# Nine warm-up products, the last LayerNorm shared by three engines, and the third residual scale in quarters behind FFN2's groups 2 to 5

## The chip, the cores and the metric

The kernel runs on one NeuronCore of a Trainium2 chip. The metric is the device time of one execution in microseconds (us). Engines are named as in the profile: PE is TensorE, DVE is VectorE, ACT is ScalarE, POOL is GpSimd, SP is SyncE, which here only issues DMAs. L246 is line 246 of the kernel; lines behind 380 shift by 3 to 8 in the changed kernel.

## The reference

One layer on 256 tokens of width 2048, in float32. Four blocks follow each other, each with a residual and a LayerNorm behind it:

```python
h = LN(alpha*h + 0.5*SwiGLU_1(h))                  # D_FF = 5504
h = LN(alpha*h + mixer(h))                         # chunked attention and latent attention, gated
h = LN(alpha*h + CrossAttn(h, LN(mem)))            # 4 heads, 256 memory tokens
h = LN(alpha*h + 0.5*SwiGLU_2(h))

def layer_norm(x, g, b):
    mu = x.mean(-1); var = square(x - mu).mean(-1)
    return (x - mu) * rsqrt(var + 1e-5) * g + b
```

## The kernel before, in words

**Products in float32 by halves.** Every float32 operand is split into a rounded half `hi` and a rest `lo`, both of a type that PE takes at full pace. A product is three passes: hi with hi, hi with lo, lo with hi. A weight is loaded in pieces of 128x2048 (1 MB) into one of three raw buffers (`raw`, L182, issued on SP), ACT casts it to `hi` (L243, in pieces of 1024 columns), DVE subtracts to form `lo` (L246). There are two buffers each of `hi` and `lo`; `load` and `halves` (L195 to L247) do this. Activations stand transposed (`T`, `H`, `X` blocks), in halves too, formed by `split` (L235 cast, L236 subtract). A part of the steps is done with sums of weight blocks and of activation blocks, seven products in place of eight (`mm_sums`, L354; the weight sums are L190 and L192 on DVE, from raw into a block named H or X, then cast and subtracted into an X block; the activation sums `sum_forms`, L310 and L314).

**Order.** Steps are put in a list with `add`, each with its weights and a priority; `run` goes through the list, loads weights some steps ahead and emits the instructions. A scheduler then orders each engine's instructions by dependencies and priority: SOON (400) goes ahead of its place in the program, LATE (-400) behind it. On the chip each engine runs its list in that order, and a waiting instruction holds all behind it on its engine.

**FFN.** Eleven groups of 512 hidden columns (the last has 384). A group is eight steps of two 128-row pieces of the input: pairs (L300, 24 products of 512 columns) and sums (L354, 21 products). Gate and up of both token halves fill four PSUM banks; `hidden` (L693) multiplies them, and its `turn` transposes the result on PE (L705) within the next group, whence ACT and DVE bring it to an H block (L235, L236). Groups alternate between the bank pools `mm` and `at`; a group with sums uses banks of both. The first half (groups 0 to 5) is followed by its part of the output projection (`out_pair`), then come groups 6 to 10 and the rest. FFN2's group 0 (`first_group`) is cut up, since the LayerNorm ahead of it comes in between: gate of both halves first, then four `up` steps (L287).

**The residual.** h stands in two tiles (h0, h1), one for each 128 tokens. A LayerNorm writes its normalised h, without scale and offset, back to h, and the transposed form with scale and offset to the T blocks. The scale and offset of the residual itself follow later in `gb_apply` (L434 to L446): for each quarter of 512 columns two row vectors are loaded over all partitions by DMAs of POOL into two of the five 128x512 work tiles `w2`, and DVE multiplies (L445) and adds (L446) for both token halves: four DVE operations of 128x512 and two DMAs a quarter. There are three such passes; the third, `gb_apply(2)`, lies in FFN2 and has to be done before FFN2's output is added.

**Start.** `start` (L470 on) issues 12 products of 128x128 on a tile of ones (L476, results unused), then the first eight steps of FFN1, whose weights and inputs arrive in small pieces.

**End.** The last columns of FFN2's output are made for token half 0, then half 1 (`out_proj` with `cut`; L749, L750, L759). `final_steps` normalises a half: statistics, 1/root by a start value and three steps on 128x1 values (`rsqrt`, L362 to L367), then for each quarter (h - mean)*g (L1361) and *r + b (L1362) on DVE, and the store (L1363) by ACT or SP. Half 0 is done while PE makes half 1; half 1 stands alone at the end.

Of the kernel before, what the change touches and what calls it, by code (L numbers as in the profile page):

```python
# [46 lines left out]
SOON, NEAR, LATE = 400, 100, -400  # L47
WARM = 12
HEADS = ("H4", "H5", "X2", "X3")
# [42 lines left out]
class Kernel:  # L92
# [286 lines left out]

    def ln_scale(self, st):  # L380
        nc = self.nc
        mv, v, y, a = (self.sm(k, n, bufs=2) for k, n in (("mv", 2), ("v", 1), ("y", 1), ("a", 1)))
        nc.vector.bn_aggr(mv, st)
        nc.vector.tensor_scalar(v, mv[:, 1:2], LN_EPS, None, ALU.add)
        self.rsqrt(v, y, a)
        nb = self.sm("nb", 1, bufs=2)
        self.chain = nc.vector.scalar_tensor_tensor(nb, mv[:, 0:1], -1.0, y, ALU.mult, ALU.mult)
        return mv[:, 0:1], y, nb
# [136 lines left out]
    def ffn(self, tag, xT, st, first=None, steps=None, late=None, before=None, tags=None):  # L525
# [6 lines left out]
        for half, nf in enumerate(F_SPLIT):  # L532
# [3 lines left out]
            for g in range(-(-nf // 4)):  # L536
# [15 lines left out]
                hidden, turn = self.hidden(ps, bank, g, n, hid, qs)  # L552
                self.add(hidden, prio=SOON)
                if j == 0 and first is not None:
                    for c in SUMS_IN:
                        self.add(self.forms_step(fx, SUMS_IN, c, xT))
# [93 lines left out]
    def first_group(self, tag, xT, before, ps, fx):  # L650
# [18 lines left out]
        for g in range(4):  # L669
# [5 lines left out]
            self.add(fn, t[tag + "_up"][0, :, g * 2048:(g + 1) * 2048])  # L675
            if g == 0:
                self.add(lambda: self.gb_apply(2, self.h), prio=LATE)
            else:
                self.add(self.forms_step(fx, SUMS_IN, tuple(SUMS_IN)[g - 1], xT))
# [42 lines left out]
    def out_proj(self, wname, nk, x, scale, st, steps=None, tags=None, n0=0, other=False, cut=False):  # L722
# [13 lines left out]
        def part(n, tts, i, ps, tags=None, held=0, keep=False, again=False):  # L736
            grp = groups[i]

            def fn(w=None):
# [12 lines left out]
                for tt in tts:  # L752
# [4 lines left out]
                    if short:  # L757
                        hs = h[tt][:, n * 512:(n + 1) * 512]
                        nc.vector.tensor_tensor(hs, hs, ps[tt], ALU.add)  # L759
                if i == len(groups) - 1:  # L760
# [584 lines left out]
    def final_steps(self, st):  # L1345
# [8 lines left out]
        def steps(tt):  # L1354
            def fn():
                mean, r, _ = self.ln_scale(st[tt])
                g, b = e["gb"]
                for q in range(4):
                    cs = slice(q * 512, (q + 1) * 512)
                    hs = h[tt][:, cs]  # L1360
                    nc.vector.scalar_tensor_tensor(hs, hs, mean, g[:, cs], ALU.subtract, ALU.mult)  # L1361
                    nc.vector.scalar_tensor_tensor(hs, hs, r, b[:, cs], ALU.mult, ALU.add)  # L1362
                    (nc.sync if q % 2 else nc.scalar).dma_start(self.out[0, tt * P:(tt + 1) * P, cs], hs)  # L1363
# [140 lines left out]
```

## Time and profile before

| | us |
|---|---|
| median of 3 runs (2484.69 to 2485.30) | 2485.29 |
| the profiled execution | 2485.13 |
| its span, first to last instruction | 2483.4 |
| PE busy, share of the span | 2467.4, 99% |
| DVE busy | 2066.2, 83% |
| ACT busy | 1337.6, 54% |
| POOL busy | 31.8, 1% |

The profile is of one execution. A timeline row has the start, the duration, the engine, the line, the operation, written tile <- read tiles (buffer numbers left out), the shape and a count when like instructions are merged; behind it stands the idle time of the engine before the row and what ended it. The duration of a merged row reaches from the first start to the last end. Neighbours on one engine overlap by some 0.07 us, so DVE's 128x512 operations of 0.68 us follow each other every 0.6. A row of groups has the busy time, the mean of one in ns, and the idle time before. A row of windows has the length, the busy time of each engine shown with its count, the granted clock of PE, the DMA share and GB/s.

### The profile page before, as it was taken

How to read it: one execution, taken by the hardware profiler on the slowest of the kernel's cores; microseconds unless marked ns; L12 is line 12 of the kernel's file. 1: busy time of each engine (PE TensorE's matmuls, PEld its weight loads, DVE VectorE, ACT ScalarE, POOL GpSimd, SP SyncE). 2: the span in 40 equal slices, each digit the busy share in tenths (PEclk: the TensorE clock that was granted, in tenths of full speed). 3: DMA queues.
4: the chain of work that ended last, by engine and by line, in shares of the span. 5: the costliest groups of instructions: out<-in, count | busy, mean ns of one | idle time of the engine just before them, and what ended most of it. 6: DMA issues, size and time to landing. Idle time of an engine off the chain costs nothing.

```text
span 2483.4 us, 30482 instructions
## 1 busy us (share of the span) xinstructions
PE 2467.4 (99%) x11953; PEld 2079.9 (84%) x11953; DVE 2066.2 (83%) x2334; ACT 1337.6 (54%) x1803; POOL 31.8 (1%) x75
## 2 busy tenths in 40 slices
PE   9999999999999999999999999999999999999998
PEld 8888888889888888899888888888888888888886
DVE  6999889899778988677688798557888988898986
ACT  5555555555455555555455565545545555555552
POOL 0000000000000001000000000000000000000000
PEclk9999999999999999999999999999999999999999
DMA  7655556555645656554566547544655555655663
GB/s 259 240 196 204 187 200 211 203 187 204 237 155 210 212 203 219 178 163 141 172 235 217 189 174 248 189 155 150 209 197 187 203 187 204 210 198 202 203 216 140
DMA packets 72945, 490.16 MB, mean 197 GB/s; under 512 B 8449, under 2 KB 8961, under 8 KB 17633
## 3 DMA queue, kind: packets, MB, share of 16 engines
q1 hardware_dynamic: 67200, 468.29, 54.3%
q0 software_dynamic: 4448, 18.09, 2.2%
q8 instruction: 93, 1.52, 0.2%
q10 hardware_dynamic: 1152, 1.84, 0.2%
q14 instruction: 52, 0.42, 0.0%
HBM read 484.77 MB, written 2.10 MB: 196 GB/s over the span
## 4 chain that ended last, share of the span: by engine, by line
PE 93%; DVE 3%; DMA 2%; ACT 1%; issue 1%; DVEq 0%; ACTq 0%
PE mm L300 26%; PE at L300 24%; PE mm L354 10%; PE at L354 10%; PE mm L266 7%; PE mm L287 5%; PE mm L268 4%; PE mm L256 2%; DVE lo L246 1%; PE at L963 1%; DMA raw<-ffn_w_out_r 1%; PE at L802 1%; DMA raw<-w_xo_r 1%; PE at L1320 0%; PE at L405 0%
## 5 line engine op out<-in xcount | busy, mean ns | idle before, releaser
L243 ACT CAST hi<-raw 128x1024 fp32r<-128x1024 f32 (+1 forms) x848 | 800.9, 986 | 586.1 <-PE at L300 170.5
L246 DVE TENSOR_TENSOR lo<-raw,hi 128x2048 fp32r<-128x2048 f32 (+2 forms) x425 | 902.8, 2125 | 225.0 <-ACT hi L243 220.6
L300 PE MATMUL mm<-hi,T 128*128 128x512 f32 (+1 forms) x1280 | 298.2, 383 | 0.0
L243 ACT CAST X<-H 128x1024 fp32r<-128x1024 f32 (+1 forms) x162 | 165.0, 1034 | 220.4 <-DVE H L192 87.6
L300 PEld LDWEIGHTS mm<-hi,T 128*128 128x128 f32 x1280 | 238.3, 188 | 44.1 <-DVE H L833 0.3
L300 PE MATMUL at<-hi,T 128*128 128x512 f32 x1072 | 257.0, 389 | 0.0
L246 DVE TENSOR_TENSOR X<-H,X 128x2048 fp32r<-128x2048 f32 (+1 forms) x81 | 182.3, 2250 | 67.6 <-ACT X L243 67.6
L300 PEld LDWEIGHTS at<-hi,T 128*128 128x128 f32 x1072 | 201.1, 188 | 41.9
L300 PE MATMUL mm<-lo,T 128*128 128x512 f32 (+1 forms) x640 | 153.8, 382 | 0.0
L300 PE MATMUL at<-hi,H 128*128 128x512 f32 x592 | 140.7, 390 | 0.0
L300 PEld LDWEIGHTS mm<-lo,T 128*128 128x128 f32 x640 | 119.1, 188 | 21.8
L300 PE MATMUL at<-lo,T 128*128 128x512 f32 x536 | 132.6, 389 | 0.0
L300 PEld LDWEIGHTS at<-hi,H 128*128 128x128 f32 x592 | 110.9, 188 | 23.0 <-DVE w L647 0.2
L266 PE MATMUL mm<-T,hi 128*128 128x512 f32 x512 | 124.0, 393 | 0.0
L300 PEld LDWEIGHTS at<-lo,T 128*128 128x128 f32 x536 | 100.6, 188 | 20.9
L300 PE MATMUL mm<-hi,H 128*128 128x512 f32 x464 | 112.3, 392 | 0.0
L192 DVE TENSOR_TENSOR H<-H,raw 128x512 f32<-128x512 f32 (+1 forms) x162 | 109.3, 675 | 1.7
L266 PEld LDWEIGHTS mm<-T,hi 128*128 128x128 f32 x512 | 93.8, 188 | 19.3 <-issue 0.9
L300 PEld LDWEIGHTS mm<-hi,H 128*128 128x128 f32 x464 | 86.2, 188 | 17.6 <-DVE w L275 0.2
L190 DVE TENSOR_TENSOR H<-raw 128x1024 f32<-128x1024 f32 (+1 forms) x81 | 97.1, 1198 | 3.6 <-DMA raw<-ffn_w_in 2.4
L354 PE MATMUL mm<-X,X 128*128 128x512 f32 x348 | 95.7, 391 | 1.7 <-DVE H L236 1.7
L243 ACT CAST X<-raw 128x1024 fp32r<-128x1024 f32 (+1 forms) x54 | 55.3, 1036 | 52.1 <-DVE raw L192 31.5
(332 smaller groups left out, 3946.6 us busy)
## 6 DMA issues: line engine op xcount, KB each, us to landing
raw<-ffn_w_in SPq DMA_DIRECT2D x150, 1024.0 KB, 4.8
raw<-ffn_w_out SPq DMA_DIRECT2D x66, 1024.0 KB, 4.8
raw<-w_gate SPq DMA_DIRECT2D x32, 1024.0 KB, 4.9
raw<-ffn_w_out_r SPq DMA_DIRECT2D x16, 1024.0 KB, 4.9
raw<-w_qk SPq DMA_DIRECT2D x16, 1024.0 KB, 4.8
raw<-w_o_b SPq DMA_DIRECT2D x16, 1024.0 KB, 4.8
raw<-w_out SPq DMA_DIRECT2D x16, 1024.0 KB, 4.8
raw<-w_xk SPq DMA_DIRECT2D x16, 1024.0 KB, 5.0
```

Of the source, the lines that this page charges most:

```text
L190: self.nc.vector.tensor_tensor(two[0], two[1], raw[:, :m].unsqueeze(1).to_broadcast([P, 2, m]), ALU.add)
L192: self.nc.vector.tensor_tensor(t[:, a * m:a * m + m], t[:, b * m:b * m + m], raw[:, a * m:a * m + m], ALU.add)
L243: self.nc.scalar.copy(hi[:, c:d], src[:, c:d])
L246: self.nc.vector.tensor_tensor(lo[:, :n], src, hi[:, :n].bitcast(F32), ALU.subtract)
L256: self.nc.tensor.matmul(ps, w[wi][:, cols[j]:cols[j] + P], x.at(xi, kt), start=(j + wi + xi == 0), stop=(j == n - 1 and wi == 1),)
L266: self.nc.tensor.matmul(ps, hi[kt], x.both(kt), start=(kt == 0), stop=False)
L268: self.last_mm = self.nc.tensor.matmul(ps[:, :S], lo[kt], x.at(0, kt), start=False, stop=(kt == n - 1))
L287: self.last_mm = self.nc.tensor.matmul(ps, x.at(xi, kt)[:, tt * P:(tt + 1) * P], w[wi][:, j * 512 + c:j * 512 + c + m], start=(start and j ...
L300: self.last_mm = self.nc.tensor.matmul(ps[tt, g][:, :n], x.at(xi, kt)[:, tt * P:(tt + 1) * P], w[wi][:, c:c + n], start=first and j + wi + ...
L354: self.last_mm = self.nc.tensor.matmul(bank[:, :m], a[xi], v[wi][:, c * m:(c + 1) * m], start=own and first and wi + xi == 0, stop=own and ...
L802: self.nc.tensor.transpose(ps[:, i * P:(i + 1) * P], s[:, c:c + P], self.ident)
L963: nc.tensor.matmul(ps[:, c0:c0 + nk], q[:, tt * P:(tt + 1) * P], k[:, :nk], start=(j == 0), stop=(j == len(parts) - 1))
```

## The change

Four edits:

- `WARM` goes from 12 to 9.
- `gb_apply(2)` is no longer one step in FFN2's group 0; its four quarters are four steps, each LATE, behind the hidden product of groups 2, 3, 4 and 5.
- In the last LayerNorm the quarters run in the order 2, 3, 0, 1. For token half 1 the quarters 0 and 1 get their (h - mean) from ACT (with -mean as bias) and their *g from POOL; DVE keeps that for 2 and 3, and all four *r + b. -mean is formed ahead of the root, in place of -mean/root behind it, which is unused there.
- The addition of a short product in `out_proj` gets the priority SOON.

```diff
-WARM = 12
+WARM = 9
...
-    def ln_scale(self, st):
+    def ln_scale(self, st, plain=False):
...
         nc.vector.bn_aggr(mv, st)
+        nb = self.sm("nb", 1, bufs=2)
+        if plain:
+            nc.vector.tensor_scalar(nb, mv[:, 0:1], -1.0, None, ALU.mult)
         nc.vector.tensor_scalar(v, mv[:, 1:2], LN_EPS, None, ALU.add)
         self.rsqrt(v, y, a)
-        nb = self.sm("nb", 1, bufs=2)
-        self.chain = nc.vector.scalar_tensor_tensor(nb, mv[:, 0:1], -1.0, y, ALU.mult, ALU.mult)
+        if not plain:
+            self.chain = nc.vector.scalar_tensor_tensor(nb, mv[:, 0:1], -1.0, y, ALU.mult, ALU.mult)
...
                 self.add(hidden, prio=SOON)
+                if before and 2 <= j < 6:
+                    self.add(lambda q=j - 2: self.gb_apply(2, self.h, (q,)), prio=LATE)
...
-            if g == 0:
-                self.add(lambda: self.gb_apply(2, self.h), prio=LATE)
-            else:
+            if g:
                 self.add(self.forms_step(fx, SUMS_IN, tuple(SUMS_IN)[g - 1], xT))
...
                         hs = h[tt][:, n * 512:(n + 1) * 512]
-                        nc.vector.tensor_tensor(hs, hs, ps[tt], ALU.add)
+                        with self.prio(SOON):
+                            nc.vector.tensor_tensor(hs, hs, ps[tt], ALU.add)
...
-                mean, r, _ = self.ln_scale(st[tt])
+                mean, r, nm = self.ln_scale(st[tt], bool(tt))
                 g, b = e["gb"]
-                for q in range(4):
+                for q in (2, 3, 0, 1):
                     cs = slice(q * 512, (q + 1) * 512)
                     hs = h[tt][:, cs]
-                    nc.vector.scalar_tensor_tensor(hs, hs, mean, g[:, cs], ALU.subtract, ALU.mult)
+                    if tt and q < 2:
+                        nc.scalar.activation(hs, hs, AF.Identity, bias=nm)
+                        nc.gpsimd.tensor_tensor(hs, hs, g[:, cs], ALU.mult)
+                    else:
+                        nc.vector.scalar_tensor_tensor(hs, hs, mean, g[:, cs], ALU.subtract, ALU.mult)
                     nc.vector.scalar_tensor_tensor(hs, hs, r, b[:, cs], ALU.mult, ALU.add)
```

What the scheduler makes of it, at three places. First DVE in FFN2's group 0, just behind the last pieces of the transposed LayerNorm (T blocks); h_102 and h_103 are the residual's two halves, w the work tiles. Before:

```order
L236 TENSOR_TENSOR T_2187_14256<-w_2211_14428,T_2187_14256 128x4x128
L414 TENSOR_SCALAR w_2213_14441<-at_14436,vecs 128x128
L445 TENSOR_TENSOR h_102<-h_102,w_2226_14556 128x512
L445 TENSOR_TENSOR h_103<-h_103,w_2226_14556 128x512
L236 TENSOR_TENSOR T_2188_14257<-w_2213_14441,T_2188_14257 128x4x128
L446 TENSOR_TENSOR h_102<-h_102,w_2227_14557 128x512
L446 TENSOR_TENSOR h_103<-h_103,w_2227_14557 128x512
L246 TENSOR_TENSOR lo_14476<-raw_14473,hi_14475 128x2048
L445 TENSOR_TENSOR h_102<-h_102,w_2228_14564 128x512
L246 TENSOR_TENSOR lo_14495<-raw_14492,hi_14494 128x2048
L446 TENSOR_TENSOR h_102<-h_102,w_2229_14565 128x512
```

The same place now:

```order
L236 TENSOR_TENSOR T_2187_14253<-w_2211_14425,T_2187_14253 128x4x128
L417 TENSOR_SCALAR w_2213_14438<-at_14433,vecs 128x128
L314 TENSOR_TENSOR w_2231_14586<-w_2230_14585 128x128 x2
L314 TENSOR_TENSOR w_2231_14586<-w_2231_14586,w_2230_14585 128x128
L310 TENSOR_TENSOR w_2235_14625<-T_2187_14253 128x512
L236 TENSOR_TENSOR T_2188_14254<-w_2213_14438,T_2188_14254 128x4x128
L314 TENSOR_TENSOR w_2231_14586<-w_2230_14585,w_2231_14586 128x128
L314 TENSOR_TENSOR w_2236_14626<-w_2235_14625 128x128 x2
L314 TENSOR_TENSOR w_2236_14626<-w_2236_14626,w_2235_14625 128x128
L310 TENSOR_TENSOR w_2246_14675<-T_2188_14254 128x512
L246 TENSOR_TENSOR lo_14473<-raw_14470,hi_14472 128x2048
```

The sixteen operations on h are gone from there, and the activation sums (L310, L314) have moved ahead of the weights' lo.

Second, DVE in the group behind group 2, now, from the split of its hidden turn (H_2364) on; H_2363 and H_2379 are weight sums:

```order
L236 TENSOR_TENSOR H_2364_15403<-mm_15411,H_2364_15403 128x4x128
L192 TENSOR_TENSOR H_2363_15399<-H_2363_15399,raw_15397 128x512
L246 TENSOR_TENSOR lo_15444<-raw_15397,hi_15443 128x1536
L448 TENSOR_TENSOR h_102<-h_102,w_2349_15320 128x512
L246 TENSOR_TENSOR X_2374_15449<-H_2363_15399,X_2373_15448 128x2048
L246 TENSOR_TENSOR lo_15480<-raw_15477,hi_15479 128x2048
L190 TENSOR_TENSOR H_2379_15486<-raw_15484 128x1024
L246 TENSOR_TENSOR lo_15512<-raw_15484,hi_15511 128x1536
L192 TENSOR_TENSOR H_2379_15486<-H_2379_15486,raw_15484 128x512
L449 TENSOR_TENSOR h_102<-h_102,w_2350_15321 128x512
L192 TENSOR_TENSOR H_2379_15486<-H_2379_15486,raw_15484 128x512
L448 TENSOR_TENSOR h_103<-h_103,w_2349_15320 128x512
```

One more L449 and the next X follow. L448 and L449 are L445 and L446 of before; without these four rows the order there is that of before. Behind groups 3 and 5 it is much the same, behind group 4 two L448 stand ahead of the turn's splits.

Third, the end of DVE, token half 1, from the aggregate of the statistics (mv) on. Before:

```order
L384 TENSOR_SCALAR v_19428<-mv_19427 128x1
L1361 SCALAR_TENSOR_TENSOR h_103<-h_103,mv_19427,T_2876_18715 128x512
L362 TENSOR_SCALAR y_19429<-v_19428 128x1
L1361 SCALAR_TENSOR_TENSOR h_103<-h_103,mv_19427,T_2876_18715 128x512
L363 TENSOR_SCALAR v_19428<-v_19428 128x1
L1361 SCALAR_TENSOR_TENSOR h_103<-h_103,mv_19427,T_2876_18715 128x512
L366 TENSOR_SCALAR a_19430<-y_19429,v_19428 128x1
L1361 SCALAR_TENSOR_TENSOR h_103<-h_103,mv_19427,T_2876_18715 128x512
L367 TENSOR_SCALAR y_19429<-a_19430,y_19429 128x1
```

Now:

```order
L386 TENSOR_SCALAR nb_19429<-mv_19424 128x1
L387 TENSOR_SCALAR v_19425<-mv_19424 128x1
L1369 SCALAR_TENSOR_TENSOR h_103<-h_103,mv_19424,T_2876_18712 128x512
L362 TENSOR_SCALAR y_19426<-v_19425 128x1
L1369 SCALAR_TENSOR_TENSOR h_103<-h_103,mv_19424,T_2876_18712 128x512
L363 TENSOR_SCALAR v_19425<-v_19425 128x1
L366 TENSOR_SCALAR a_19427<-y_19426,v_19425 128x1
L367 TENSOR_SCALAR y_19426<-a_19427,y_19426 128x1
```

Two of the four big operations have left DVE, and nb stands in front. Behind the root four L1370 (L1362 of before) follow in both. The two products are the last work on POOL, and on ACT two activations (L1366) stand between the stores of half 0 and those of half 1. The short addition (L759, now L763) keeps its place behind the four L1370 of half 0.

## The prediction, made before the changed kernel was run

> **What bounds the kernel now.** I read the page first: the engines' shares and the chain that ended last.
>
> ```profile
> span 2483.4 us, 30482 instructions
> PE 2467.4 (99%) x11953; PEld 2079.9 (84%) x11953; DVE 2066.2 (83%) x2334; ACT 1337.6 (54%) x1803; POOL 31.8 (1%) x75
> PE 93%; DVE 3%; DMA 2%; ACT 1%; issue 1%; DVEq 0%; ACTq 0%
> ```
>
> TensorE (PE) is busy for all but 16.0 us of the span. What can be won lies in those 16 us, or in PE instructions that go; what can be lost is any new wait of PE. So the second view is what PE waited for in the whole run (us in total, times, longest).
>
> ```profile
> PE mm L354 <- DVE H L236: 1.7, 1, 1.7
> PE at L476 <- DVE w L452: 1.1, 1, 1.1
> ```
>
> The other waits of PE are 0.6 us and less. Third, the timeline at three places. At the start PE runs the warm-up products and then its first real ones; at the end DVE alone runs the last LayerNorm after PE has stopped at about 2471.7; the 1.7 us wait stands in FFN2. The change touches exactly these three. The sum below is against the profiled execution: span 2483.4, own time 2485.13, which lies 0.16 below the median of 2485.29; the 1.8 us around the span stay.
>
> **Warm-up, 12 products to 9.**
>
> ```profile
> 1.06 5.49 PE L476 MATMUL at<-w 128*128 128x128 f32 x24 [1.06 <-DVE w L452]
> 4.89 1.19 ACT L235 CAST hi<-raw 128x512 fp32r<-128x512 f32 x2 [2.20 <-DMA H<-xT]
> 6.21 0.70 PE L300 MATMUL mm<-hi,T 128*128 128x512 f32 x1
> 6.74 1.09 PE L300 MATMUL mm<-hi,T 128*128 128x512 f32 x4
> 11.99 3.79 PE L300 MATMUL mm<-hi,T 128*128 128x512 f32 x16
> 60.96 1.03 PE L705 MATMUL mm<-ident,w 128*128 128x128 f32 x8
> ```
>
> Twelve products are 24 records, from 1.06 to the first real product at 6.21: 0.21 us each. Products of the same shape later (L705) come 0.11 apart, so PE runs at half pace here. The first real product takes 0.70 us and the next four 1.09 together: full pace came between 6.2 and 6.74. Three products less free 6 x 0.21 = 1.28 us. They are not all gained: the first weights (hi) are ready only when the first of the two casts ends, at 4.89 + 0.6 = 5.5. The products start at about 5.57, not 4.93, so 0.64 us come free, and at half pace they hold half as much work: **0.33 us**. The next inputs come in time for that: the second cast ends at 6.1, needed at 6.6, and the later pieces of the first two units keep 0.2 us or more. From 11.99 on PE runs without a gap, so the 0.33 lasts. Nothing to zero is the other end if the pace rises earlier, since the last warm-up products are then short.
>
> **The third scale and offset (L445, L446) out of FFN2's first group.**
>
> ```profile
> L446 DVE TENSOR_TENSOR h<-h,w 128x512 f32<-128x512 f32 x8 | 5.3, 683 | 0.6 <-DMA w<-gb 0.6
> L445 DVE TENSOR_TENSOR h<-h,w 128x512 f32<-128x512 f32 x8 | 5.2, 682 | 0.0
> 1815.29 1.07 PE L287 MATMUL mm<-lo,T 128*128 128x512 f32 x4
> 1815.99 0.62 ACT L235 CAST X<-w 128x512 fp32r<-128x512 f32 x1 [3.53 <-DVE w L314]
> 1820.94 2.29 DVE L246 TENSOR_TENSOR lo<-raw,hi 128x2048 fp32r<-128x2048 f32 x1 [2.37 <-ACT hi L243]
> 1823.26 0.33 SPq L182 DMA_DIRECT2D raw<-ffn_w_in  x1
> 1829.27 1.23 DVE L190 TENSOR_TENSOR H<-raw 128x1024 f32<-128x1024 f32 x1 [2.42 <-DMA raw<-ffn_w_in]
> 1836.16 1.98 PE L300 MATMUL at<-lo,T 128*128 128x512 f32 x8
> 1841.85 0.39 PE L354 MATMUL mm<-X,X 128*128 128x512 f32 x1
> 1843.19 1.28 DVE L236 TENSOR_TENSOR H<-mm,H 128x512 fp32r<-128x512 f32 x2
> 1843.93 1.66 PE L354 MATMUL mm<-X,X 128*128 128x512 f32 x6 [1.69 <-DVE H L236]
> ```
>
> Between 1795.5 and 1818.6 DVE runs these 16 operations, 10.5 us, and 0.6 us of waiting for their loads. They stand ahead of the sums that ACT waits for (3.53 us), so ACT casts the weights of the last `up` step late, DVE forms their lo late (1820.94), the raw buffer comes free late and the load on SP goes out at 1823.26. DVE then idles 2.42 us for that load and runs without a pause from 1829.27 to the split L236 at 1843.19, whose PSUM bank PE wants 0.23 after 1841.85. That is PE's 1.7 us.
>
> Without the 16 operations the lo at 1820.94 is bound by PE alone. Its buffers come free near 1816.3, when PE ends the step two before (the row at 1815.29), so I put its end at 1820, 3.2 us earlier. The load follows, L190 starts at 1826 to 1826.5, the next lo ends near 1831, and its load is back for the second L190 near 1836. The lo ahead of L236 needs a buffer that PE gives back at 1838.1 (the row at 1836.16); then 2.2 us of it, and the first L236 ends near 1841.5. PE wants the bank at 1842.1. What is late next is that same split, with some 0.6 us to spare: I take **1.7 us** gained, bounds 0 and 1.85 (the whole gap of 2.08 between the two products less the usual 0.23).
>
> **The same operations behind groups 2 to 5.** Four per group, in DVE's pace 4 x 0.6 = 2.4 us. DVE's busy time from one hidden turn to the next:
>
> ```profile
> 1924.80:1967.20 42.40, 39.17 (x39) 1.00 0.56 198
> 1967.20:2009.65 42.45, 38.37 (x34) 1.00 0.60 204
> 2009.65:2052.10 42.45, 38.76 (x38) 1.00 0.50 172
> 1935.03 2.29 DVE L246 TENSOR_TENSOR X<-H,X 128x2048 fp32r<-128x2048 f32 x1 [0.90 <-ACT X L243]
> 1944.77 2.29 DVE L246 TENSOR_TENSOR X<-H,X 128x2048 fp32r<-128x2048 f32 x1 [1.12 <-ACT X L243]
> 1950.25 2.29 DVE L246 TENSOR_TENSOR lo<-raw,hi 128x2048 fp32r<-128x2048 f32 x1 [0.98 <-ACT hi L243]
> 1949.53 0.62 PE L354 MATMUL at<-X,T 128*128 128x512 f32 x2
> ```
>
> Idle are 3.2 to 4.1 us of each group, for 2.4 us of work, and the order puts the work where the idle stands. Behind group 2 the first L445 falls into the 0.90 us before the X at 1935.03. One L446 between the two L192 delays the second by 0.6 us, hence ACT's cast of X and the X at 1944.77 by 0.6. PE reads that X's lo half after 1949.5, when it had been done at 1947.1: 1.8 us are left. The 0.98 us before the lo at 1950.25 take up the rest. So **0**, with the idle as cover; without it 4 x 2.4 = 9.6 us. What stands behind a late L445 on DVE are lo and X, which PE and, through the raw buffer, SP's loads wait for. The loads g and b go out on POOL as before, now two per group. In group 2 the first waits for the turn near 1925 to free its buffer, nine us ahead of its L445; a DVE wait there is possible only in the last quarter, where L446 follows the freed buffer by a few us.
>
> **The tail.**
>
> ```profile
> 2472.80 0.29 DVE L383 BATCH_NORM_AGGREGATE mv<-bn 128x2 f32<-128x30 f32 x1
> 2473.19 0.74 DVE L1361 SCALAR_TENSOR_TENSOR h<-h,mv,T 128x512 f32<-128x512 f32 x1
> 2474.58 0.14 DVE L363 TENSOR_SCALAR v<-v 128x1 f32<-128x1 f32 x1
> 2476.14 0.20 DVE L367 TENSOR_SCALAR y<-a,y 128x1 f32<-128x1 f32 x1
> 2477.25 0.21 DVE L367 TENSOR_SCALAR y<-a,y 128x1 f32<-128x1 f32 x1
> 2477.57 2.73 DVE L1362 SCALAR_TENSOR_TENSOR h<-h,y,T 128x512 f32<-128x512 f32 x4
> L895 ACT ACTIVATE H<-H,ly 128x512 f32<-128x512 f32 x2 | 1.3, 716 | 2.0 <-DVE ly L371 2.0
> L462 POOL MEMSET krope<- 128x512 f32 x1 | 0.5, 515 | 0.0
> masks.py:199 POOL TENSOR_SCALAR_AFFINE_SELECT ident<-ident 128x128 f32<-128x128 f32 x1 | 0.3, 285 | 0.0
> ```
>
> DVE keeps two L1361 and loses two. The two that go stood between the small steps of the root and hid their latency, so less than 2 x 0.66 is won. The new nb in front costs 0.07. v at L363 then stands at 2474.65, its two successors 0.2 and 0.3 later, so the first y of the loop at 2475.15 in place of 2476.14. The last y is 1.11 after it (2476.14 to 2477.25), at 2476.26, and with the old nb gone L1362 starts at 2476.51 in place of 2477.57: 1.06 us. Each L1362 and its store follow as before (0.66 apart, the store 2.1 us from issue to landing), so the end moves as much, if quarters 0 and 1 are ready as third and fourth, by 2477.8 and 2478.5. ACT gets nb at 2473.3 and needs some 0.72 each (L895): 2474.1 and 2474.8. It has nothing queued ahead but the first half's stores, issued by then. POOL multiplies after that. Its product of two inputs stands in no row. Below: a 128x512 memset takes 0.515, so not less; above: the 128x128 select with one input takes 0.285, so four times that for each of two inputs, 2.3. By one pass of 0.41 per stream, two in and one out, it is 0.1 + 3 x 0.41 = 1.3, near the lower rows, and I take 1.3: done at 2475.4 and 2476.7, in time, **1.06**. If POOL and DVE's L1361 and L1362 cannot run beside each other, POOL starts at 2474.7, ends at 2477.3, and the first L1362 waits until then: 0.24 is left. No row shows the two side by side, so I take the middle, **0.65**. At 2.3 each and in turns POOL would end at 2479.3 and DVE at 2482.0: 1.8 lost.
>
> The Trainium skill speaks against this part: "SBUF — State Buffer", section "SBUF: two separate sides", says that a GpSimd operation that reads SBUF and a DVE operation with two SBUF inputs share a port pair as an exclusive lock for the whole instruction. By that rule the tail gives 0.24 and the sum is 2.3; no run here shows it yet.
>
> SOON around the short add moves nothing: DVE's order has that add behind the same four L1362.
>
> **Sum.** 0.33 + 1.7 + 0 + 0.65 = 2.7 us; 2485.1 - 2.7 = **2482.5**.
>
> **Rivals.**
> First, the clock. Full pace may need an unbroken run of PE, and the change leaves a gap of 0.64 us at 4.9. The profile records that idleness takes the pace away:
>
> ```profile
> 2471.70:2474.50 2.80, 0.03 (x1) 0.00 (x0) 2.70 (x8) 0.00 (x0) 0.00 (x0) 1.00 0.13 48
> 2474.50:2480.00 5.50, 0.00 (x0) 0.00 (x0) 5.32 (x15) 0.00 (x0) 0.00 (x0) 0.50 0.15 55
> ```
>
> The granted clock (third from the right) is 0.50 some 2.8 us after PE's last product. Before, full pace came 5.1 to 5.7 us after the first product. Counted anew from 5.57 it comes near 11.1 in place of 6.7, and half of 4.4 us, 2.2, is lost: 2484.7. Against it: PE waited 1.7 us in FFN2 and kept its pace. Chance 20%. The Trainium skill, "TensorE: Matmul & The Clock Gate", Part 1, has a free-running window of about 3.4 us that must be busy; by it one window more costs 1.7 us, 2484.2. The 5.1 to 5.7 us of half pace here agree with one window missed and one kept.
>
> Second, the split L236 stays late in FFN2, since DVE's run of nearly 14 us ahead of it has the same instructions: 1.7 us are not won, 2484.2. The 2.42 us of idle that go speak against it. 10%.
>
> Third, POOL is slow and takes turns with DVE: the tail loses 1.8 instead of gaining 0.65, 2484.9. 12%.
>
> Fourth, on the other side: DVE's late lo and X reach PE in groups 2 to 5. With none of the 9.6 us covered the time is 2482.5 + 9.6 = 2492.1; from 2.7 us uncovered on, the kernel is slower than before. For it: DVE is 90 to 92% busy there, and its idle is itself a wait for ACT, which waits for DVE. Against: no PE wait stands in these groups now, and the slack counted above. 4%.
>
> **The numbers.** The forecast has 54%, with 2481.9 (all bounds good) to 2483.7 as its own range. The range that should hold 8 in 10 takes in the first three rivals: 2481.4 to 2484.9. A measurement of this kernel tells about 0.2% from no change, here 5 us: below 2480.3 lies none of the cases (2% for what I overlook), above 2490.3 only the fourth (4%), so 94% within.
>
> **What would show it.** Right: 18 warm-up records, the first L300 product at 5.5 to 5.6 and its row of 16 at about 11.65 in place of 11.99; no PE wait on L236 near 1841; no PE wait in groups 2 to 5; the last L1362 ending some 7.9 us after PE's last product instead of 8.6. Wrong: L300 rows still 0.43 apart after 7 us, a PE wait on lo or X in FFN2, an idle DVE before the third L1362 with POOL as its releaser.

## The result, and the profile after

The changed kernel takes **2482.48 us** (median of 22 runs, 2481.79 to 2483.96) beside 2485.61 for the kernel before (22 runs, 2483.86 to 2488.49): ratio 0.9986, 95% interval 0.9981 to 0.9992. That is 3.1 us; 2482.5 had been predicted, as 2.7 us less than a before of 2485.1. The profiled execution took 2481.91, its span is 3.3 us shorter than the one of before. From here on, offsets are starts of the same instruction in the two profiles, after less before. Each profile is of one execution.

The page after the change, span, PE and the chain that ended last; then what PE waited for.

```profile
span 2480.1 us, 30475 instructions
PE 2466.1 (99%) x11947; PEld 2078.3 (84%) x11947; DVE 2065.5 (83%) x2332; ACT 1338.7 (54%) x1805; POOL 34.8 (1%) x77
PE 96%; DVE 2%; DMA 1%; ACT 0%; issue 0%; SPq 0%; DVEq 0%; ACTq 0%
```
```profile
PE at L479 <- DVE w L455: 1.1, 1, 1.1
PE mm L300 <- ACT hi L235: 0.7, 2, 0.6
```

The row for the 1.7 us wait on the split L236 is gone. A new wait stands in L300, on hi: that is at the start. PE there, then ACT:

```profile
1.06 3.92 PE L479 MATMUL at<-w 128*128 128x128 f32 x18 [1.06 <-DVE w L455]
5.56 2.96 PE L300 MATMUL mm<-hi,T 128*128 128x512 f32 x10 [0.58 <-ACT hi L235]
8.69 1.66 PE L300 MATMUL mm<-hi,T 128*128 128x512 f32 x6 [0.17 <-ACT hi L235]
12.00 3.79 PE L300 MATMUL mm<-hi,T 128*128 128x512 f32 x16
```
```profile
7.11 0.62 ACT L235 CAST hi<-raw 128x512 fp32r<-128x512 f32 x1 [1.08 <-DMA raw<-ffn_w_in]
8.01 0.62 ACT L235 CAST hi<-raw 128x512 fp32r<-128x512 f32 x1 [0.28 <-DMA raw<-ffn_w_in]
```

The first product starts 0.65 us earlier, but the row of 16 begins at 12.00 (before: 11.99). The next pieces of hi come when their loads land, and PE waits for both casts: of the ten merged products one starts at 7.78, and the row of six at 8.69, each 0.05 to 0.06 us after the end of a cast (7.73, 8.63). **Nothing is gained here.** Full pace came earlier in this execution than in the one of before: the last warm-up records, from 4.6 on, are 0.11 us apart, so the first real products ran at full pace, and all that this and the earlier start gave went into these waits and smaller pauses beside them.

FFN2's first groups, DVE and then PE:

```profile
1825.79 1.22 DVE L190 TENSOR_TENSOR H<-raw 128x1024 f32<-128x1024 f32 x1
1836.17 1.22 DVE L190 TENSOR_TENSOR H<-raw 128x1024 f32<-128x1024 f32 x1 [1.16 <-DMA raw<-ffn_w_in]
1840.97 1.28 DVE L236 TENSOR_TENSOR H<-mm,H 128x512 fp32r<-128x512 f32 x2
```
```profile
1841.71 0.73 PE L354 MATMUL mm<-X,X 128*128 128x512 f32 x2
1843.90 2.44 PE L300 MATMUL at<-hi,T 128*128 128x512 f32 x10
```

The splits are at 1840.97 in place of 1843.19, and PE's product at 1841.71 comes only 0.1 late. It is still that split that releases it: the weight load that goes with it waits for the split, and starts 0.05 us after its end at 1841.66.

```profile
1841.71 0.30 PEld L354 LDWEIGHTS mm<-X,X 128*128 128x128 f32 x2 [0.38 <-DVE H L236]
```

The offset goes from 0.00 at 1838 to -1.76 at 1843.9.

DVE and PE behind groups 2, 3 and 4, as windows that lie within 0.4 us of those before (length, PE, PEld, DVE, ACT, POOL, granted clock, DMA share, GB/s):

```profile
1923.40:1965.85 42.45, 42.45 (x194) 35.22 (x193) 41.60 (x43) 24.43 (x31) 1.08 (x2) 1.00 0.59 210
1965.85:2008.30 42.45, 42.45 (x193) 35.09 (x192) 41.80 (x40) 23.72 (x30) 1.07 (x2) 1.00 0.64 224
2008.30:2050.75 42.45, 42.45 (x193) 35.07 (x192) 39.22 (x37) 23.05 (x28) 1.08 (x2) 1.00 0.59 191
```

DVE has 2.4, 3.4 and 0.5 us more than before, and behind group 5 (2050.3 to 2092.4) 2.2 more; the fullest window leaves it 0.65 us of idle. PE is busy throughout, and the offset stays within 0.1 us from 1850 to 2100: the quarters cost nothing, with less room than before.

The tail, token half 1: ACT, POOL, DVE; then POOL's and DVE's lines by themselves (ns, shortest, median, longest).

```profile
2470.81 1.33 ACT L1366 ACTIVATE h<-h,nb 128x512 f32<-128x512 f32 x2 [17.88 <-DVE nb L386]
2471.62 2.94 POOL L1367 TENSOR_TENSOR h<-h,T 128x512 f32<-128x512 f32 x2 [119.32 <-ACT h L1366]
2470.29 0.29 DVE L383 BATCH_NORM_AGGREGATE mv<-bn 128x2 f32<-128x30 f32 x1
2471.47 0.74 DVE L1369 SCALAR_TENSOR_TENSOR h<-h,mv,T 128x512 f32<-128x512 f32 x1
2473.99 3.10 DVE L1370 SCALAR_TENSOR_TENSOR h<-h,y,T 128x512 f32<-128x512 f32 x4
```
```profile
L1367 POOL TENSOR_TENSOR h<-h,T x2: 1254/1488/1721, 2471.6 to 2473.3; 128x512 f32<-128x512 f32 x2
L1370 DVE SCALAR_TENSOR_TENSOR h<-h,y,T x4: 739/739/1114, 2474.0 to 2476.4; 128x512 f32<-128x512 f32 x4
```

From the aggregate's start to the end of the last multiply-add: 6.80 us, before 7.50 (2472.80 to 2480.30), so **0.70 gained**. POOL's first product, begun while DVE's second L1369 ran, took 1.72, the second 1.25; DVE's first L1370, begun 0.56 us before POOL's second ended (at 2474.56), took 1.11 in place of 0.74.

A fourth place had not been in the prediction: the last loads of FFN2's output. Before, with the DMA view of the first 4 us behind the issue at 2444.52 (queue, kind: packets, MB, share; then the load's KB and time to landing):

```profile
2450.10 1.05 ACT L243 CAST X<-raw 128x1024 fp32r<-128x1024 f32 x1 [3.62 <-DMA raw<-ffn_w_out_r]
2451.06 1.99 ACT L243 CAST hi<-raw 128x1024 fp32r<-128x1024 f32 x2
2453.08 2.29 DVE L246 TENSOR_TENSOR lo<-raw,hi 128x2048 fp32r<-128x2048 f32 x1 [3.67 <-ACT hi L243]
2455.42 1.21 PE L287 MATMUL mm<-lo,H 128*128 128x512 f32 x4 [0.33 <-DVE lo L246]
```
```profile
q8 instruction: 1, 0.02, 1.9%
raw<-ffn_w_out_r SPq DMA_DIRECT2D x1, 1024.0 KB, 5.6
```

And after, the same load, issued at 2442.68:

```profile
2447.56 1.05 ACT L243 CAST X<-raw 128x1024 fp32r<-128x1024 f32 x1 [2.93 <-DMA raw<-ffn_w_out_r]
```
```profile
q1 hardware_dynamic: 127, 1.02, 75.6%
raw<-ffn_w_out_r SPq DMA_DIRECT2D x1, 1024.0 KB, 4.9
```

Before, the load landed 5.6 us after its issue, a transfer of 16 KB of the kind "instruction" fell into its first 4 us, and PE lost 0.6 us from 2454.7 on (gaps of 0.49 and 0.11 beyond the usual spacing): ACT's cast to X waits for the load, its casts to hi stand behind that one, DVE's lo waits for hi, and PE for lo. After, the transfer falls 4.4 us behind the issue, when the load is nearly done; the load takes 4.9 and PE does not wait. The account of the profiled pair: 0 + 1.76 + 0 + 0.6 + 0.70 = 3.06, and 0.2 us of scatter between.

### The profile page after: what moved, and what is told of

It reads as the page before. It is cut to its first block, busy times and chain, and to the rows that moved or that the text cites. A ratio compares the mean times of both kernels' runs of the same rounds, so it can differ in the third digit from the quotient of the medians.

```text
span 2480.1 us, 30475 instructions
## 1 busy us (share of the span) xinstructions
PE 2466.1 (99%) x11947; PEld 2078.3 (84%) x11947; DVE 2065.5 (83%) x2332; ACT 1338.7 (54%) x1805; POOL 34.8 (1%) x77
## 4 chain that ended last, share of the span: by engine, by line
PE 96%; DVE 2%; DMA 1%; ACT 0%; issue 0%; SPq 0%; DVEq 0%; ACTq 0%
PE mm L300 26%; PE at L300 25%; PE mm L354 10%; PE at L354 10%; PE mm L287 7%; PE mm L266 7%; PE mm L268 4%; PE mm L256 2%; PE at L967 1%; PE at L287 1%; PE at L806 1%; PE at L1324 0%; PE at L408 0%; PE at L1300 0%; PE at L1008 0%; PE mm L708 0%
## 5 line engine op out<-in xcount | busy, mean ns | idle before, releaser
L300 PE MATMUL mm<-hi,T 128*128 128x512 f32 (+1 forms) x1280 | 298.7, 383 | 0.8 <-ACT hi L235 0.7
L300 PEld LDWEIGHTS mm<-hi,T 128*128 128x128 f32 x1280 | 237.8, 188 | 46.0 <-ACT hi L235 2.1
L300 PE MATMUL at<-hi,T 128*128 128x512 f32 x1072 | 257.0, 389 | 0.0
L300 PEld LDWEIGHTS at<-hi,T 128*128 128x128 f32 x1072 | 201.1, 188 | 41.9
L300 PE MATMUL mm<-lo,T 128*128 128x512 f32 (+1 forms) x640 | 153.8, 382 | 0.0
L300 PE MATMUL at<-hi,H 128*128 128x512 f32 x592 | 140.7, 389 | 0.0
L300 PEld LDWEIGHTS mm<-lo,T 128*128 128x128 f32 x640 | 119.1, 188 | 21.8
L300 PE MATMUL at<-lo,T 128*128 128x512 f32 x536 | 132.6, 389 | 0.0
L300 PEld LDWEIGHTS at<-hi,H 128*128 128x128 f32 x592 | 110.9, 188 | 22.9
L300 PEld LDWEIGHTS at<-lo,T 128*128 128x128 f32 x536 | 100.6, 188 | 20.9
L300 PE MATMUL mm<-hi,H 128*128 128x512 f32 x464 | 112.3, 392 | 0.0
L300 PEld LDWEIGHTS mm<-hi,H 128*128 128x128 f32 x464 | 86.2, 188 | 17.6 <-DVE w L275 0.2
L190 DVE TENSOR_TENSOR H<-raw 128x1024 f32<-128x1024 f32 (+1 forms) x81 | 97.2, 1200 | 2.1 <-DMA raw<-ffn_w_in 1.2
```

The lines of the kernel that those rows point to most:

```text
L190: self.nc.vector.tensor_tensor(two[0], two[1], raw[:, :m].unsqueeze(1).to_broadcast([P, 2, m]), ALU.add)
L300: self.last_mm = self.nc.tensor.matmul(ps[tt, g][:, :n], x.at(xi, kt)[:, tt * P:(tt + 1) * P], w[wi][:, c:c + n], start=first and j + wi + ...
```

## The experiments

All times are medians of 11 runs, differences are to the kernel before on the same chip (33 runs, 2485.80 for the first eight, 2486.01 for the last four). The 95% interval of each ratio reaches about 0.09% to either side, 2.2 us, so single edits are told apart by their profiles; the times have only to agree with them. The changed kernel stands at -3.1.

### The three parts alone

**Nine warm-up products alone.**

```diff
-WARM = 12
+WARM = 9
```

> The kernel before with 9 warm-up products in place of 12, nothing else. Theory A (the prediction's): 0.33 us faster than before, the row of 16 L300 products at about 11.65 in place of 11.99. Theory B (the inputs of the first units bind; read from the profile after the change, where the first product came at 5.56 but the row of 16 at 12.00): PE waits for hi casts between the first and the second unit, the row of 16 stays at 11.9 to 12.1, and the time is within 0.2 us of before. Theory C (the clock needs an unbroken run of PE): L300 rows 0.43 apart beyond 7 us, 1.7 to 2.2 us slower than before.

Measured: 2483.99, -1.8 (ratio 0.9994, 0.9985 to 1.0002). PE's row of 16 began at 12.09, as B had it, so A's gain at the start did not come, and neither did C's loss. The median fell by more than A or B had; the interval (0.5 us slower to 3.7 faster) takes in both, but PE's gains in the profile lie at places that **no theory had**. PE in FFN2, DVE's sum ahead of it, and the DMA view of the load behind that sum:

```profile
1843.49 1.67 PE L354 MATMUL mm<-X,X 128*128 128x512 f32 x6 [0.35 <-DVE H L236]
```
```profile
1828.83 1.23 DVE L190 TENSOR_TENSOR H<-raw 128x1024 f32<-128x1024 f32 x1 [1.48 <-DMA raw<-ffn_w_in]
```
```profile
raw<-ffn_w_in SPq DMA_DIRECT2D x1, 1024.0 KB, 5.0
```

The wait on the split shrank from 1.7 to 0.35 although the 16 operations were still in place: the load issued at 1823.77 landed in 5.0 us, the one of before (1823.26) in 6.0. That is 1.0 of the 1.35; the rest is that PE itself came here 0.9 us later than before and the load was issued only 0.5 later. The loss at 2454 was gone too (its load took 4.8). The profile gains 1.35 and 0.65 there, and loses 0.8 us near 690, where L405 waited 0.93 (0.17 before) after two loads that took 7.0 and 6.5 us (6.2 and 5.1 before); no 16 KB instruction transfer lies in them, and the cause stays open. So this execution is 0.9 us faster than the profiled one of before, half of what the medians say. A theory for the gains came with the last four runs.

**The quarters alone.**

```diff
+                if before and 2 <= j < 6:
+                    self.add(lambda q=j - 2: self.gb_apply(2, self.h, (q,)), prio=LATE)
...
-            if g == 0:
-                self.add(lambda: self.gb_apply(2, self.h), prio=LATE)
-            else:
+            if g:
```

> The kernel before with the third scale and offset in quarters behind FFN2 groups 2 to 5, nothing else. Theory A: it alone removes the wait of 1.7 us on the L236 split in FFN2's first groups, and costs nothing behind groups 2 to 5: 1.7 us faster than before (1.5 to 1.9), no row of PE waiting on H L236 for 1.7. Rival: the wait went for another reason (the shift of the start or of the order elsewhere) and this edit alone gives under 0.5; or the quarters cost PE something in groups 2 to 5 that the whole change hid, then PE waits on lo or X between 1840 and 2100.

Measured: 2484.30, -1.5 (0.9992, 0.9983 to 1.0001). No row of PE waiting for H L236; the offset falls from -0.07 at 1838 to -2.08 at 1843.6, so the edit removes the whole wait by itself, as theory A had it. PE was busy all through the four groups. The profile gave 1.2 back later: 0.6 at 2370, and 0.6 more than before at 2454, where the load took 6.1.

**The tail alone**: the changed kernel with `WARM = 12` and `gb_apply(2)` back in group 0.

> The kernel before with the shared last LayerNorm and the SOON of the short addition alone (12 warm-up products, the third scale and offset in FFN2's first group). Theory A: 0.7 us faster than before (7.5 to 6.8 us from the aggregate of token half 1 to the end of the last multiply-add with r and b), and the 1.7 us wait of PE on L236 is there again. Rivals: 1.06, if POOL's products cost DVE nothing; 0.24, if they and DVE's operations with two inputs take turns throughout; 0, if the end is bound by the stores of half 0.

Measured: 2484.86, -0.9 (0.9994, 0.9985 to 1.0003). From the aggregate to the last L1370 6.80 us, as in the changed kernel: 0.70 gained. PE waited 1.4 on L236 again. Theory A.

### What POOL costs DVE

**POOL's two products by g left out.** The output lacks g in these places; L1370 is L1369 here.

```diff
-                        nc.gpsimd.tensor_tensor(hs, hs, g[:, cs], ALU.mult)
```

> The changed kernel without GpSimd's two multiplications by g of quarters 0 and 1 of token half 1 (the output lacks g there). Theory A (GpSimd and DVE hold each other up): the first of the four multiply-adds takes 0.74 us in place of 1.11, the row of four 2.73 in place of 3.10, and the kernel is 0.37 us faster than the changed one. Rival: the first of the four took longer for another reason (ACT writing h, or the operation itself behind the root): the row of four stays at 3.1 and the time within 0.1 of the changed kernel.

Measured: 2482.09, -3.7 (0.9983, 0.9974 to 0.9992), 0.6 below the changed kernel's -3.1. DVE's four:

```profile
2474.64 2.74 DVE L1369 SCALAR_TENSOR_TENSOR h<-h,y,T 128x512 f32<-128x512 f32 x4
```

2.74 in place of 3.10, the first one 0.75, and 6.44 us from the aggregate to the end: 0.36 less, as theory A had it. So POOL and DVE hold each other up, and 0.36 of the 1.06 us that the prediction's sum allowed goes to that. The 0.24 us of the case in which the two cannot run beside each other at all is not what came (0.70): POOL's first product started beside DVE's second L1369 and lost about 0.5 us of the 0.6 for which both ran, which put POOL's end some 0.2 us ahead of that case, and DVE's first L1370 lost 0.37 of the 0.56 us for which it ran beside POOL. The Trainium skill, "SBUF — State Buffer", section "SBUF: two separate sides", has an exclusive lock there. The trace agrees that the two hold each other up; that the whole overlap is lost it does not show.

### What the quarters cost

**Without the third scale and offset.**

```diff
-                if before and 2 <= j < 6:
-                    self.add(lambda q=j - 2: self.gb_apply(2, self.h, (q,)), prio=LATE)
```

> The changed kernel without the third scale and offset altogether (the residual goes into FFN2's output unscaled by it; 16 operations of DVE and 8 loads less). Theory A (the quarters behind groups 2 to 5 lie in DVE's idle time): within 0.3 us of the changed kernel, DVE's busy time about 10.5 us less in those groups. Rival: they cost PE a part of their 9.6 us, and this kernel is faster by that part, over 0.5 us.

Measured: 2482.68, -3.1 (0.9987, 0.9979 to 0.9996), the same as the changed kernel, though 16 operations of DVE are missing (its busy time is 8.5 us less). From 1850 to 2100 PE's offset to before stays at -2.40, as the changed kernel's stays near -1.75: the cover is whole.

**All four quarters behind group 2.**

```diff
-                if before and 2 <= j < 6:
-                    self.add(lambda q=j - 2: self.gb_apply(2, self.h, (q,)), prio=LATE)
+                if before and j == 2:
+                    self.add(lambda: self.gb_apply(2, self.h), prio=LATE)
```

> The changed kernel with all four quarters as one late step behind group 2 in place of one each behind groups 2 to 5. Theory A (cover is the idle time of DVE in the group, 3.2 to 4.1 us, and a lag reaches PE when it exceeds that and the 1.8 us by which X is ahead): 9.6 us of work less 3.2 to 4.1 of idle less 1.8 leave 3.5 to 4.5 us of PE waiting on lo or X behind group 2, and the kernel is that much slower than the changed one. Rival B: late priority and the few work tiles spread the sixteen operations over two or more groups, and nothing is lost (within 0.3 of the changed kernel). Rival C: as in the first group of the kernel before, a late lo delays a load on SP and the wait comes one group later, about 1.7 us.

Measured: 2491.15, +5.4 (1.0021, 1.0012 to 1.0029), so 8.5 us slower than the changed kernel, twice what A had. What PE waited for, and the windows around it:

```profile
PE mm L300 <- DVE w L652: 5.1, 1, 5.1
```
```profile
1964.80:1969.90 5.10, 0.02 (x1) 0.00 (x0) 5.07 (x9) 0.00 (x0) 0.00 (x0) 0.97 0.00 0
1969.90:1973.00 3.10, 3.04 (x7) 2.48 (x8) 3.10 (x7) 1.86 (x3) 0.00 (x0) 0.50 0.00 0
1973.00:1976.00 3.00, 3.00 (x18) 2.54 (x18) 2.99 (x6) 2.82 (x5) 0.00 (x0) 1.00 0.00 0
```

The lag went to a place that A did not name: it gathered up to the end of group 3, where DVE's additions L649, L651 and L652 read PE's sums out of PSUM, and PE waited 5.1 us (and lost 0.6 near 1961) for the banks. Behind that wait the granted clock was 0.50 in the window of 3.1 us, another 1.4 us lost. This is the rival on the other side, DVE's backlog reaching PE, and it decides on where the four quarters stand, not on their sum of 9.6 us.

### The warm-up

```diff
-WARM = 9
+WARM = 0
```

> The changed kernel without warm-up products. Theory A (the clock rises only after PE has been busy for a stretch): the first real products, from 5.5 on, run 0.43 us apart for at least one window, and half of 3.4 to 5 us is lost: 1.7 to 2.5 us slower than the changed kernel. Theory B (the inputs of the first units bind and leave gaps in which half pace is hidden): 0.3 to 1.2 us slower. Rival: warm-up does nothing, within 0.2 us.

> The changed kernel with 5 warm-up products in place of 9 (they end near 3.2 us, 2.3 us ahead of the first hi). Theory A (full pace needs a busy stretch that reaches up to the first real product): half pace from 5.5 on for a window, 1 to 2 us slower than the changed kernel. Theory B (2.1 us of products are enough, or the inputs bind anyway): the row of 16 L300 products at 12.0, time within 0.2 us of the changed kernel.

Measured: without warm-up 2484.03, -1.8 (0.9991, 0.9982 to 1.0); with 5 products 2485.14, -0.7 (0.9997, 0.9988 to 1.0006). The first rows of each, none first and 5 after it:

```profile
5.55 6.70 PE L300 MATMUL mm<-hi,T 128*128 128x512 f32 x16 [5.55 <-ACT hi L235]
13.93 3.79 PE L300 MATMUL mm<-hi,T 128*128 128x512 f32 x16
```
```profile
5.54 5.85 PE L300 MATMUL mm<-hi,T 128*128 128x512 f32 x16 [1.98 <-ACT hi L235]
13.04 3.79 PE L300 MATMUL mm<-hi,T 128*128 128x512 f32 x16
```

At the start 1.9 and 1.0 us are lost against the changed kernel, theory A in both; the times are 1.3 and 2.4 us above the changed kernel's, so it is the rows and not the times that tell the theories apart. The products of L300 are 0.43 us apart at first, and 0.22 from 11.6 on without warm-up, from 9.7 on with 5 products. The kernel with 5 lost more elsewhere: a load issued at 2285.8 with an instruction transfer 0.6 us behind it landed in 7.2 us, and PE waited 0.78 and 0.89 near 2295 and 2312. From 9 products to 12 the start hardly changes any more: the row of 16 lies at 11.81 to 12.07 in the four profiles with 12 (mean 11.98) and at 11.54 to 12.10 in the five with 9 (mean 11.90), 0.1 us where 0.33 had been predicted.

### Where the instruction transfers fall

**9 and 3 small ones, in the kernel before; the same in the changed kernel.**

```diff
-        for _ in range(WARM):
-            nc.tensor.matmul(warm[:, :P], self.ones, self.ones, start=True, stop=True)
+        for i in range(12):
+            n = P if i < 9 else 16
+            nc.tensor.matmul(warm[:, :n], self.ones, self.ones[:, :n], start=True, stop=True)
```

> The kernel before with 9 warm-up products of 128 columns and 3 of 16: PE has as many instructions as before, but the warm-up ends as early as with 9. In the runs so far the 16 KB transfers of queue q8 (kind instruction, 93 in each profile) lie elsewhere among the weight loads when PE has fewer instructions ahead, and a load with such a transfer 0 to 3.5 us behind its issue lands in 5.2 to 6.3 us in place of 4.8. Theory F (the 1.8 us that 9 products alone gained came from that): the transfers lie as before, PE waits 1.4 to 1.7 us on the L236 split near 1842 and 0.6 near 2454.7, and the time is within 0.4 us of before. Rival D (the shorter warm-up itself gained them): 1.5 to 1.9 us faster than before, as with 9 products alone.

> The changed kernel with three more warm-up products of 16 columns: PE has as many instructions as with 12. Theory F: the load of ffn_w_out_r issued near 2442.7 lands in 5.6 us or more in place of 4.3, PE waits 0.5 to 1.1 us near 2453, no wait comes back near 1842, and it is 0.5 to 1.1 us slower than the changed kernel. Rival D: the same as the changed kernel within 0.3 us.

**9 wide ones in the kernel before; the changed kernel with 12.**

```diff
-        self.ones = self.w1((P, P))
+        self.ones = self.w1((P, 170))
...
-        for _ in range(WARM):
-            nc.tensor.matmul(warm[:, :P], self.ones, self.ones, start=True, stop=True)
+        for _ in range(9):
+            nc.tensor.matmul(warm[:, :170], self.ones[:, :P], self.ones, start=True, stop=True)
```

> The kernel before with 9 warm-up products of 170 columns: the warm-up is as long as with 12 of 128, but PE has as few instructions as with 9. Theory F: as with 9 products alone, 1.3 to 2.0 us faster than before, no wait of PE at 2454.7, under 0.5 us on the L236 split near 1842. Rival D: as before, within 0.4 us, with both waits.

> The changed kernel with 12 warm-up products, so without the first of its edits. Theory F: as with the three small ones, 0.5 to 1.1 us slower than the changed kernel, all of it behind 2440, and the row of 16 L300 products at 11.8 to 12.1 as ever. The prediction's working: 0.33 us slower, with that row 0.33 later than in the changed kernel. Rival D, with the start bound by its inputs: no difference, within 0.2 us.

| | time (to before) | load near 2444: time to landing, instruction transfer in its first 4 us | PE's loss there | wait on L236 |
|---|---|---|---|---|
| before, 12 | 2485.6 | 5.6, one | 0.6 | 1.7 |
| before, 9 | -1.8 | 4.8, none | 0 | 0.35 |
| before, 12, quarters alone | -1.5 | 6.1, one | 1.2 | 0 |
| before, 12, tail alone | -0.9 | 5.6, one | 0.6 | 1.4 |
| before, 9 and 3 small | +0.8 | 6.2, one | 1.2 | 1.9 |
| before, 9 wide | -2.1 | 5.1, none | 0.1 | 0.8 |
| changed, 9 | -3.1 | 4.9, none | 0 | 0 |
| changed, 9 and 3 small | -2.6 | 6.0, one | 1.1 | 0 |
| changed, 12 | -2.8 | 6.0, one | 1.0 | 0 |

The changed kernel with 12, PE's row and its load, as one of these:

```profile
2454.32 1.21 PE L287 MATMUL mm<-lo,H 128*128 128x512 f32 x4 [0.76 <-DVE lo L246]
```
```profile
q8 instruction: 1, 0.02, 1.5%
raw<-ffn_w_out_r SPq DMA_DIRECT2D x1, 1024.0 KB, 6.0
```

**Theory F holds for the place** in all nine rows: with PE's instruction count of 12 products an instruction transfer lies in the first 4 us of that load, with the count of 9 none does, and 9 wide ones are like 9. The five profiles of the sections above with 9, 5 or no products have none there either (4.8 to 5.0 us). At 1823 it is the same: 6.0, 6.0 and 6.3 us with one (12; 9 and 3 small; tail alone), 5.0 and 5.2 without (9; 9 wide), which moves the wait on L236.

The traces hold more than these two loads. Counted in PE's real products, the 93 transfers of the six kernels with 12 warm-up products' instructions start at the same places, with a scatter of 3 products. With the instructions of 9 they come 5 products later in the mean, with 5 products 13 and without warm-up 24, and 6, 14 and 24 PE records were taken away. And of the loads of 1 MB in the profile of before, from 100 us on, the 26 with such a transfer in their first 4 us took 5.7 us to landing (median), the 384 others 4.8; in the other 13 profiles the medians are 5.2 to 6.0 and 4.8.

The times say less. Only the 2.8 us between 9 wide and 9 and 3 small, run on one chip, stand out of the intervals; the 0.3 and 0.5 us by which the changed kernel is slower with 12, or with 3 small ones more, do not (F had 0.5 to 1.1), and rest on the profiles. Four marks against a clean reading: the +0.8 of 9 and 3 small is outside F's 0.4, and its waits of 1.9 and 1.2 us are above F's 1.7 and 0.6. (The 4.3 us that the expectation for the changed kernel has as the load's time to landing should be 4.9.) Its profile is of the slowest of its 11 runs (2490.0, median 2486.8), so what it lost beyond the table's places is not typical of it. The small products were no shorter: they came 0.21 us apart like the others at half pace, so in the kernel before that run repeats the warm-up of 12 rather than shortening it; in the changed kernel, where full pace came earlier, the first product stood at 5.53 as with 9, and the loss at 2454 was back all the same. So it is this last run that parts F from D: its start is that of 9 products, its loss that of 12. And the wait on L236 with 9 wide ones, 0.8, is above the 0.5 that F had, and their warm-up was no longer than that of 9 in its effect, the first product standing at 5.64 and not at 6.2.

That slowest execution of 9 and 3 small showed one more thing. Its windows from the wait on L236 on (the third from the right is the granted clock):

```profile
1844.60:1846.10 1.50, 0.31 (x1) 0.30 (x2) 1.50 (x3) 0.00 (x0) 0.00 (x0) 1.00 0.52 87
1846.10:1849.50 3.40, 3.40 (x9) 2.64 (x8) 1.90 (x2) 1.38 (x2) 0.00 (x0) 0.50 0.89 306
1849.50:1852.00 2.50, 2.50 (x12) 2.03 (x11) 1.86 (x1) 0.61 (x1) 0.00 (x0) 1.00 0.88 367
```

Here the 1.9 us wait was followed by 3.4 us at a granted clock of 0.50, 1.6 us of further loss; the 1.7 us wait of before was not. In each trace the changes of the granted clock lie whole multiples of 3.413 us apart, 723 of them (2467.84 us) in the one of before. On that grid the wait that cost the pace lay inside one stretch, from 1842.69 to 1846.10, and that of before lay across the end of one at 1843.05, 0.8 us on one side and 0.9 on the other; so it can be the place of a wait as well as its length that counts. In the same profile the products at the start stayed 0.43 apart up to 9.7, with 24 warm-up records as before, and 1.5 us were lost; why the pace rose so late there is open. The Trainium skill, "TensorE: Matmul & The Clock Gate", Part 1, has a free-running window of about 3.4 us; the 3.4 us agree with it.

## Why the prediction was right, point by point

- **Warm-up, 0.33: the size and the mechanism failed.** "The later pieces of the first two units keep 0.2 us or more" was wrong: PE waited for the hi casts at 7.11 and 8.01, and the row of 16 stayed at 12.00 (0.1 over all profiles). Nor did the first products run at half pace in that profile. The edit gained all the same, 0.6 us in the profiled pair, at the far end of the kernel, by a mechanism that the prediction did not have: three products fewer are six PE records fewer, and they move PE's instruction transfers out of a load that PE waits for. In the medians that is 0.3 us, inside the interval.
- **FFN2, 1.7: right** (1.76). The first L190 came at 1825.8 (1826 to 1826.5 was said), the first split ended at 1841.7 (1841.5). The 0.6 us to spare behind it were not there: PE wanted the bank at 1841.6, and waited 0.1. Two edits act on the same wait: nine products alone took 1.35 of it, the quarters alone all. The parts' times alone (1.8, 1.5, 0.9) add to 4.2 and not to 3.1, but with 2.2 us of interval on each this shows nothing; their profiled spans are 1.0, 1.0 and 0.6 below the one of before.
- **The wait's cause was told incompletely.** The chain from the 16 operations to the late load is right, as their removal shows; but 1.0 us of the 1.7 was the load's own 6.0 us in place of 5.0.
- **Quarters, 0: right**; without them the time is the same. What it rests on is the spread over four groups: in one place they cost 8.5 us.
- **Tail, 0.65: right** (0.70). The middle was a choice between two cases, so that the number came so near is luck; that POOL and DVE hold each other up in part, 0.36 us of 1.06, is what the runs show. The 1.3 us taken for POOL's product was 1.25, though its parts (0.1 and three times 0.41) stood in no row.
- **Clock rival: not seen in the changed kernel**, but its profile does not test it, since full pace came at 4.6, ahead of the gap. The profile with all four quarters behind group 2, which has the same nine products, does: its products were 0.42 us apart up to 6.9, the gap stood ahead of them, and full pace came then and not near 11. The rival's place was named too narrowly: with 9 products the start survives, with 5 or none it loses 1.0 and 1.9, and FFN2's wait can cost the clock (1.6 us in one execution).
- **The other rivals did not come**: the split was not late, POOL's second product was done 0.6 us after DVE's first L1370 began and ahead of the third and fourth, and PE waited for nothing in groups 2 to 5. (The third rival's loss adds up to 1.7, not 1.8.)
- So 2482.5 was met with one term at zero and one unforeseen gain of 0.6, and with a before that measured 2485.61 in place of 2485.29. That the forecast and the median agree to 0.02 us is luck; the fall of 2.7 that was forecast was 3.1.

## What to carry to other kernels

When PE is busy for 99% of the span, look at each load that PE waits for behind a cast: here a transfer of PE's own instructions in its first 4 us went with about 1 us more, and a change of a few PE instructions far ahead moved it in or out, so a small edit's effect may lie nowhere near the edit. Before adding up single edits, see which of them act on the same wait. Idle time of an engine covers work only where it stands: spread over four groups the 16 operations were free, in one they cost PE 8.5 us.

## What the runs showed of the hardware that was not expected

- Each profile has 93 transfers of 16 KB of the kind instruction on queue q8 and some 50 smaller ones on q14. In the loads near 2444 and 1823 one such transfer in the first 4 us went with 5.6 to 6.3 us to landing, and 4.8 to 5.2 without. That q8 carries PE's instructions is inferred, from how the 93 transfers move with the number of PE's instructions (5, 13 and 24 products later for 6, 14 and 24 records fewer).
- POOL's product of two 128x512 inputs took 1.25 us, and 1.72 when it started beside a DVE operation that reads two such inputs; DVE's, started 0.56 us before POOL's end, took 1.11 in place of 0.74. All eight profiles with these products have it within 0.01 us.
- A wait of 1.9 us of PE was followed by 3.4 us at half pace in one profile, a wait of 1.7 us in another was not; the first lay inside one stretch of the 3.413 us grid on which the granted clock changes, the second across two.
- At half pace a product of 16 columns took as long as one of 128 (0.21 us per record), with a weight block of 128x128 ahead of each.
